# A hybrid attention/SSD block on one core: two gate tiles and two projection tiles computed by halves of 512 tokens, with attention's output loaded a run ahead

## The chip, the cores and the metric

The kernel runs on one core of a Trainium2 chip. The metric is the device time of one execution in microseconds (us). Five engines run in parallel, each through its own list of instructions in order: PE (TensorE, matrix products; PEld is its weight load), ACT (ScalarE), DVE (VectorE), POOL (GpSimd) and SP (SyncE, which here only issues DMA transfers). Engines wait for each other by semaphores.

## The reference

One block over 1024 tokens of width 1024. What matters here is the mixer: a combined input projection feeds an attention branch, an SSD (Mamba-2) branch and two gates; the attention branch's output is projected, gated and merged with the other branch's.

```python
h = rmsnorm(x, pre_norm_mix) * (1.0 + scale_m) + shift_m
proj = h @ w_in
q_lat, kv_lat, k_idx, w_idx, z, xbc, dt_raw, g_a, g_b = jnp.split(proj, IN_SPLITS, axis=-1)
y_a = sparse_mla_attention(q_lat, kv_lat, k_idx, w_idx, positions, ...) @ w_o_attn
y_b = ssd_mixer(z, xbc, dt_raw, ...) @ w_o_ssd
mix = (jax.nn.sigmoid(g_a) * y_a + jax.nn.sigmoid(g_b) * y_b) @ w_out
x = x + gate_m * rmsnorm(mix, post_norm_mix)
```

A feed-forward sub-layer follows.

## The kernel before

Everything is held transposed: 128 features on the partitions, 512 tokens (a half, `b` = 0 or 1) along a row. A product in float32 is made of three products of reduced-precision parts: each operand x is split into hi (ACT rounds it, a copy to float32r) and lo = x - hi (DVE or POOL subtracts). So a tile of 128 outputs by 512 tokens over 1024 inputs is 24 matmuls, called a run here: eight pieces k of the input, three matmuls each. Its weights come in two pieces of four k (`wraw`, loaded by SP; `whi`, ACT; `wlo`, POOL), from a stream W with four buffers of `wraw` and three each of `whi` and `wlo`. A second, single-buffered set `uraw`, `uh`, `ul` (`small_weights`) holds attention's small weights.

The SSD scan goes over 8 groups g and 4 chunks c. Each step (c, g) has four parts of input (`ssd_in`) and, one step later, three of output (`ssd_out`). SP loads `ld` (B, C and x), `al` (the decays) and `zy` (z and d_ea); ACT makes exponentials of `al` and `M`; PE computes `pcb`; DVE masks it (`cbm`) and multiplies `al` and `M` by it; PE transposes x and B (`px`, `pbn`), then does `pyd`, `pst` and `pyo`; DVE and POOL finish `zy`; SP stores it to `d_y`. `ld`, `al` and `zy` share eight buffers (R), so that an `ld` may have to wait until a `d_y` has landed.

Between these parts PE takes steps of six matmuls from a filler, `beside()` (L1124). It first makes eight gate tiles (t = 0 to 7: product `pw`, evicted by ACT to `g`, stored to `d_gb`), from the split input h (`Hs`, in the 32 buffers H), and then attention's projection, eight tiles (product `poa`, evicted by DVE to `ya`, stored to `d_ya`). The projection's input, attention's output `d_att`, is loaded by `at_load` (L1128): SP loads `atl` into one of nine buffers EV, ACT makes `ath`, DVE or POOL the low part, also called `atl`. Four of half 0's eight pieces go to buffers Q; the other four and all of half 1 take over H from h, where they must wait until the gates have read it. PE's order is fixed as the code is written (`in_order`); on the other engines a scheduler sorts by the time at which it expects each instruction's inputs.

Before, the order of runs is gate 6 half 0, gate 6 half 1, gate 7 half 0, gate 7 half 1, then projection tile 0 half 0, tile 0 half 1, and so on. `at_load` stands in the code before gate 7 (four pieces) and after it (twelve).

Of the kernel before, what the change touches and what calls it, by code (L numbers as in the profile page):

```python
# [11 lines left out]
F32R = mybir.dt.float32r  # L12
BF = mybir.dt.bfloat16
AF = mybir.ActivationFunctionType
OP = mybir.AluOpType
# [5 lines left out]
KT = D // P  # L21
# [17 lines left out]
POA_BOTH = 5  # L39
AT_IN_Q = 4  # L40
# [26 lines left out]
def build(tc, a, dbg=None, stop=99, slots=None):  # L67
    nc = tc.nc
    V, S, G, T, SP = nc.vector, nc.scalar, nc.gpsimd, nc.tensor, nc.sync
# [7 lines left out]
    H_ = Arena(ctx, tc, "H", n_slots["H"], 512)  # L77
    Q = Arena(ctx, tc, "Q", n_slots["Q"], 512)
    R = Arena(ctx, tc, "R", n_slots["R"], 1024)
    EV = Arena(ctx, tc, "EV", n_slots["EV"], 512)  # L80
# [4 lines left out]
    def bank_d(name):  # L85
        return pd.tile([P, 512], F32, name=name, tag="d", bufs=3)

    def bank(name):
        return ps.tile([P, 512], F32, name=name, tag="s", bufs=5)

    def f(x):
        return x.bitcast(F32)

    def half(b):
        return slice(512 * b, 512 * b + 512)

    BS = (0, 1)
# [3 lines left out]
    def dump(key, ap, idx=None):  # L101
        if dbg is not None and key in dbg:
            d = dbg[key] if idx is None else dbg[key][idx]
            SP.dma_start(d, ap)
# [19 lines left out]
    def behind(ins):  # L124

        i = ins.ins
        if i.engine in barrier:
            tc.add_manual_dep(i, barrier[i.engine], mybir.DependencyInfo(
                mybir.DependencyClass.NoSync, mybir.DependencyReason.DATA), reason="behind")


    class Stream:
# [21 lines left out]
        def next(self):  # L154
            self.used += 1
            while len(self.tiles) < min(self.used - 1 + self.ahead, len(self.q)):
                self.load()
            return self.tiles[self.used - 1]

    W = Stream("w", 4, n_slots["raw"], n_slots["hi"], n_slots["lo"], n_slots["hi"] - 1)  # L160
    def small_weights(src):

        raw, hi, lo = (wp.tile([P, 4, P], dt, name=tag, tag=tag, bufs=1)
                       for tag, dt in (("uraw", F32), ("uh", F32R), ("ul", F32R)))
        behind(SP.dma_start(raw, src))
        behind(S.activation(hi, raw, AF.Copy))
        behind(G.tensor_tensor(lo, raw, f(hi), op=OP.subtract))
        return hi, lo

    def col_tile(w):  # L170

        kt = w.shape[1]
        return [(w[:, k:k + min(4, kt - k)], min(4, kt - k)) for k in range(0, kt, 4)]
# [27 lines left out]
    d_gb = dr.tile([KT, P, L], F32, name="d_gb")  # L201
    d_att = dr.tile([KT, P, L], F32, name="d_att")
    d_ya = dr.tile([KT, P, L], F32, name="d_ya")
# [25 lines left out]
    def dense_steps(o, b, w, xs, n=6):  # L229

        i = 0
        for (hi, lo), k0, ks in w:
            for j, k in enumerate(ks):
                for wt, xi in ((hi, 0), (hi, 1), (lo, 0)):
                    T.matmul(o, wt[:, k0 + j, :], xs[k][xi][b], start=i == 0, stop=i == 23)  # L235
                    i += 1
                    if i % n == 0 and i < 24:
                        yield

    def wpieces(ks, n=4):  # L240

        return [(W.next(), 0, ks[i:i + n]) for i in range(0, len(ks), n)]

    def split_to(src, hi, lo, lo_eng=None):
        S.activation(hi, src, AF.Copy)  # L245
        (lo_eng or V).tensor_tensor(lo, src, f(hi), op=OP.subtract)  # L246

    def split(alloc, src, name, shape=None, lo_eng=None):
        hi = alloc(name + "h", shape, F32R)
        lo = alloc(name + "l", shape, F32R)  # L250
        split_to(src, hi, lo, lo_eng)
        return hi, lo
# [70 lines left out]
    rx, Hs, first = [None, None], [([None, None], [None, None]) for _ in range(KT)], {}  # L323
# [15 lines left out]
    def k_load(k):  # L339
        raw = EV("p1raw", (P, 3, P))  # L340
        SP.dma_start(raw, a["w_p1"][k])
        ts = [R(f"ada{k}", (P, 4, 256)) for _ in range(2)]
        for i in range(2):
            last = SP.dma_start(ts[i], a["ada_p"][k][i])
        first[k] = ts, raw
        return last
# [9 lines left out]
    def k_h(k, b):  # L356
        x = X0[k][b]
        V.tensor_tensor(x, x, rx[b], op=OP.mult)
        hi, lo = H_(f"h{k}h", dt=F32R), H_(f"h{k}l", dt=F32R)
        i1 = S.activation(hi, x, AF.Identity, bias=mod[:, k:k + 1], scale=amul[:, k:k + 1])  # L360
        V.tensor_scalar(x, x, amul[:, k:k + 1], mod[:, k:k + 1], op0=OP.mult, op1=OP.add)
        i2 = (G if b else V).tensor_tensor(lo, x, f(hi), op=OP.subtract)
        if k == 5:
            barrier.update((i.ins.engine, i.ins.name) for i in (i1, i2))
        Hs[k][0][b], Hs[k][1][b] = hi, lo
        dump("h", x, (k, slice(None), half(b)))

    def k_mm(k, b):
        for i, (wi, xi) in enumerate(((0, 0), (1, 0), (0, 1))):
            for t in range(3):  # L370
                T.matmul(pp1[t][b], first[k][wi][:, t, :], Hs[k][xi][b], start=k == 0 and i == 0, stop=k == KT - 1 and i == 2)
# [14 lines left out]
    with in_order(*ORDERED):  # L386
# [7 lines left out]
        S.activation(rx[0], pr0, AF.Copy)  # L394
        pp1 = [[(bank if t or b else bank_d)(f"pp{t}") for b in BS] for t in range(3)]
        k_h(0, 0)
        k_ada(1)
        x_squares(1, range(4), sums[1])
        k_mm(0, 0)
        k_mod(1)  # L400
        k_h(1, 0)
        x_squares(1, range(4, 8), sums[1])
        k_mm(1, 0)
# [5 lines left out]
        S.activation(rx[1], pr1, AF.Copy)  # L409
        k_mod(2)  # L410
        k_h(0, 1)
        k_h(1, 1)
        k_mm(0, 1)
        k_mm(1, 1)
        for k in range(AHEAD, KT):
            k_h(k, 0)
            k_h(k, 1)
            if k < KT - 1:
                i = k_load(k + 1).ins
# [14 lines left out]
    ks8 = list(range(8))  # L434
# [27 lines left out]
    for b in BS:  # L462
# [5 lines left out]
        hi, lo = Q("ksh", dt=F32R), Q("ksl", dt=F32R)  # L468
# [7 lines left out]
    dt = con.tile([P, NT, 32], F32, name="dt")  # L476
# [77 lines left out]
    for c in range(8):  # L554
# [5 lines left out]
        for hh in range(2):  # L560
            o, oo = 64 * hh, 64 - 64 * hh
            qs = []
            for b in BS:
                t = Q("qs", dt=F32R)
# [35 lines left out]
    for x in range(2):  # L600
# [3 lines left out]
        for j in range(NT):  # L604
# [3 lines left out]
            t = Q("v")  # L608
# [107 lines left out]
    if dbg is not None and "mk" in dbg:  # L716
        for i in MK:
            n = (i + 1) * P
            t = R("t")
# [237 lines left out]
    def gate_steps(c, dst):  # L957

        W.plan(col_tile(a["w_in"][c]))
        w = wpieces(ks8)  # L960
        for b in BS:
            p = bank_d("pw")
            yield from dense_steps(p, b, w, Hs)
            t = EV("g")
            S.activation(t, p, AF.Copy)
            SP.dma_start(dst[:, half(b)], t)
            yield
# [17 lines left out]
    for kind in FILL:  # L985
        if kind == "x":
            conv_group(next(n_x))
        elif kind == "z":
            t = next(n_z)
            gate(1 + t, d_z[t], AF.Silu)  # L990
        else:
            t = next(n_a)
# [121 lines left out]
    def y_load(b, ks, places):  # L1114
        for k in ks:
            t = EV("yl")
            SP.dma_start(t, d_y[k][:, half(b)])
            where = places(k)
            yh, yw = where("yh", dt=F32R), where("yw", dt=F32R)
            S.activation(yh, t, AF.Copy, scale=col("ssd_norm", k))  # L1120
            V.scalar_tensor_tensor(yw, t, col("ssd_norm", k), f(yh), op0=OP.mult, op1=OP.subtract)
            YB[b][k] = ([yh] * 2, [yw] * 2)

    def beside():  # L1124

        AT = [([None, None], [None, None]) for _ in range(KT)]

        def at_load(b, ks, where):  # L1128
            for k in ks:
                t = EV("atl")  # L1130
                SP.dma_start(t, d_att[k][:, half(b)])
                AT[k][0][b], AT[k][1][b] = split(where, t, "at", lo_eng=G if k % 2 else V)

        for t in range(8):
            if t == 7:
                at_load(0, range(AT_IN_Q), Q)
            yield from gate_steps(57 + t, d_gb[t])
        at_load(0, range(AT_IN_Q, KT), H_)
        at_load(1, range(KT), H_)
        for ts, bs in [((t,), BS) for t in range(POA_BOTH)] + [(range(POA_BOTH, 8), (b,)) for b in BS]:  # L1140
            for t in ts:
                W.plan(col_tile(a["w_o_attn"][t]))
                w = wpieces(ks8)
                for b in bs:
                    ya = EV("ya")
                    p = bank_d("poa")
                    yield from dense_steps(p, b, w, AT)
                    V.tensor_copy(ya, p)
                    SP.dma_start(d_ya[t][:, half(b)], ya)
                    yield  # L1150
            if bs == (0,):
                y_load(0, range(12), y_place)

    def y_place(k):
        return Q if k in Y_IN_Q else H_

    filler = beside() if stop != 3 else iter(())
    with in_order(mybir.EngineType.PE):
        prev = None
        for n, s_ in enumerate([(c, g) for g in range(GROUPS) for c in range(NCH)] + [None]):  # L1160
            z = {}
            steps = ([ssd_in(*s_, z)] * 4 if s_ else []) + ([ssd_out(*prev)] * 3 if prev else [])
            k, nf = 0, 4 - n % 2
# [10 lines left out]
    if stop <= 3:  # L1174
        for k in range(16):
            for b in BS:
                t = EV("ydump")
# [333 lines left out]
    with in_order(mybir.EngineType.PE):  # L1511
        AH = a_load(0, [H_] * 16 + [Q] * 6)
        sacc = None
        for t in range(8):
            if t == 4:
                A2 = a_load(1, [Q] * 7 + [R] * 4 + [H_] * 11)
            p = bank("pfo")
# [4 lines left out]
        for t in range(7):  # L1522
            fv[1][t] = H_("fv")
            p = bank("pfo")
# [12 lines left out]
        for c in (slice(0, 256), slice(256, 512)):  # L1537
            p = bank("pfo")[:, 0:256]
# [83 lines left out]
```

## Time and profile before

| | |
|---|---|
| median of three runs | 2433.98 us (2430.88 to 2435.74) |
| profiled execution | 2434.19 us, its span 2432.4 us |
| mean granted PE clock | 0.988 |
| PE busy | 2363.3 us |
| DVE, ACT, POOL busy | 1440.5, 1227.6, 1092.3 us |

A row of a timeline gives the start (us from the span's start), the duration, the engine and the line of the kernel, the operation, output<-inputs with their shapes, and in brackets how long the engine sat idle just before and what ended that (`<-`). In SP's rows (SPq) the duration is that of the issue. A row of the DMA table ends in the median time from issue to landing. Lines in profiles are those of the kernel before.

### The profile page before, as it was taken

To read this page: it belongs to the slowest core of one execution; us is meant where nothing else is said; L and a number is where in the kernel's file an instruction comes from. 1 tells how busy PE (TensorE), PEld (TensorE's weight loads), DVE (VectorE), ACT (ScalarE), POOL (GpSimd) and SP (SyncE) were. 2 spreads that over 40 slices of the span, in tenths; PEclk is the share of its full clock that TensorE was granted. 3 is DMA by queue.
4 is the path that set the end of the run, shared out by engine and by line. 5 is a ranking of instruction groups with operands and counts; after the bars stand their busy time and mean duration, and the time that the engine had idled before them with its cause. 6 is when DMAs were issued, how large, how long until landed. Compare 5 with 4: busy or idle time off the path is not lost.

```text
span 2432.4 us, 34774 instructions
## 1 busy us (share of the span) xinstructions
PE 2363.3 (97%) x11940; PEld 1939.3 (80%) x11940; DVE 1440.5 (59%) x2852; ACT 1227.6 (50%) x2357; POOL 1092.3 (45%) x879
## 2 busy tenths in 40 slices
PE   7999999999999999999998999999999999999998
PEld 5788888888887888788876787888777888888887
DVE  4566776499656666665666774456476666542212
ACT  4346665567445555557666664544454222344432
POOL 2731112222234454552445446557576545444564
PEclk9999999999999999999998999999999999999999
DMA  7224212522213232224778775654465444354642
GB/s 271 87 87 127 70 65 75 165 94 94 98 57 96 94 101 90 92 94 144 227 231 265 232 248 194 220 197 152 158 217 169 160 152 149 119 157 144 205 148 83
DMA packets 219458, 354.37 MB, mean 146 GB/s; under 512 B 21984, under 2 KB 84112, under 8 KB 219280
## 3 DMA queue, kind: packets, MB, share of 16 engines
q1 hardware_dynamic: 218560, 351.56, 44.9%
q8 instruction: 94, 1.54, 0.3%
q14 instruction: 84, 0.69, 0.1%
q10 hardware_dynamic: 720, 0.58, 0.1%
HBM read 267.88 MB, written 87.32 MB: 146 GB/s over the span
## 4 chain that ended last, share of the span: by engine, by line
PE 54%; DVE 5%; DMA 4%; ACT 3%; issue 3%; POOL 2%; SPq 1%; DVEq 0%; POOLq 0%; ACTq 0%
PE p L1346 13%; PE pfo L1478 9%; PE pw L235 7%; PE pos L225 6%; PE plg L777 4%; PE pot L225 3%; PE po L826 2%; PE pt L810 2%; PE poa L235 2%; PE puq L225 2%; DMA d_y<-zy 1%; POOL wr L1340 1%; PE pyd L1074 1%; DMA zy<-d_ea 1%; PE pst L1079 1%
## 5 line engine op out<-in xcount | busy, mean ns | idle before, releaser
L151 POOL TENSOR_TENSOR wlo<-wraw,whi 128x512 fp32r<-128x512 f32 x248 | 341.1, 1377 | 527.3 <-ACT whi L150 455.5
L1346 PE MATMUL p<-xh,wr 128*128 128x512 f32 x880 | 275.0, 391 | 4.3 <-DVE g L1396 4.2
L150 ACT ACTIVATE whi<-wraw 128x512 fp32r<-128x512 f32 x248 | 155.0, 627 | 201.9 <-PE pos L225 43.6
L1478 PE MATMUL pfo<-a,fwh 128*128 128x512 f32 (+1 forms) x684 | 208.6, 386 | 1.0 <-DVE a L246 1.0
L1340 POOL TENSOR_TENSOR wr<-a,wr 128x512 fp32r<-128x512 f32 x110 | 152.6, 1401 | 101.9 <-ACT wr L1339 69.2
L1346 PEld LDWEIGHTS p<-xh,wr 128*128 128x128 f32 x880 | 166.4, 189 | 39.8 <-DVE g L1396 4.6
L1346 PE MATMUL p<-xl,wr 128*128 128x512 f32 x440 | 172.1, 391 | 0.0
L246 POOL TENSOR_TENSOR fwl<-fw,fwh 128x512 fp32r<-128x512 f32 x92 | 114.1, 1244 | 115.9 <-ACT fwh L245 107.3
L1478 PEld LDWEIGHTS pfo<-a,fwh 128*128 128x128 f32 x684 | 127.5, 188 | 27.9 <-DVE a L246 1.9
L789 ACT ACTIVATE lg<-lg,mx 128x256 f32<-128x256 f32 (+7 forms) x128 | 98.9, 773 | 68.0 <-DVE mx L786 67.0
L1478 PE MATMUL pfo<-a,fwl 128*128 128x512 f32 (+1 forms) x342 | 131.9, 386 | 0.0
L1339 ACT ACTIVATE wr<-a 128x512 fp32r<-128x512 f32 x110 | 67.9, 629 | 124.7 <-PE p L1346 97.0
L316 POOL TENSOR_TENSOR adaw<-adaw,cs 128x512 f32<-128x512 f32 x64 | 66.7, 1043 | 132.1 <-DMA adaw<-ada_w 101.6
L245 ACT ACTIVATE fwh<-fw 128x512 fp32r<-128x512 f32 x92 | 54.4, 593 | 124.0 <-PE pfo L1478 102.4
L1346 PE MATMUL p<-h2h,wr 128*128 128x512 f32 x352 | 111.6, 394 | 0.0
L637 ACT ACTIVATE junk<-acc,cand__2203 128x1024 bf16<-128x1024 f32 (+2 forms) x96 | 86.2, 898 | 45.8 <-DVE cand__2203 L680 29.9
L225 PE MATMUL pos<-yh,wlo 128*128 128x512 f32 x256 | 100.9, 394 | 1.4 <-POOL wlo L151 1.3
L588 DVE SCALAR_TENSOR_TENSOR acc<-rel,widx,acc 128x384 f32<-128x384 f32 (+2 forms) x90 | 87.1, 988 | 24.8 <-ACT rel L583 24.7
L583 ACT ACTIVATE rel<-prel 128x512 f32<-128x512 f32 (+3 forms) x160 | 77.1, 523 | 48.4 <-PE prel L582 44.9
L225 PE MATMUL pos<-yh,whi 128*128 128x512 f32 x256 | 100.6, 393 | 0.4 <-ACT whi L150 0.4
L225 PE MATMUL pos<-yw,whi 128*128 128x512 f32 x256 | 100.6, 393 | 0.0
L1346 PEld LDWEIGHTS p<-xl,wr 128*128 128x128 f32 x440 | 83.2, 189 | 17.3
(572 smaller groups left out, 6886.4 us busy)
## 6 DMA issues: line engine op xcount, KB each, us to landing
wraw<-w_in SPq DMA_DIRECT2D x130, 256.0 KB, 2.9
a<-w_ffn_in SPq DMA_DIRECT2D x124, 256.0 KB, 3.4
fw<-w_ffn_out SPq DMA_DIRECT2D x80, 256.0 KB, 2.7
adaw<-ada_w SPq DMA_DIRECT2D x64, 256.0 KB, 3.0
al<-d_ac SPq DMA_DIRECT2D x32, 512.0 KB, 5.9
wraw<-w_o_ssd SPq DMA_DIRECT2D x64, 256.0 KB, 3.2
al<-d_a SPq DMA_DIRECT2D x44, 256.0 KB, 5.4
d_a<-g SPq DMA_DIRECT2D x40, 256.0 KB, 2.3
```

The source lines that it names most:

```text
L150: behind(S.activation(hi[:, :kt], raw[:, :kt], AF.Copy))
L151: behind(G.tensor_tensor(lo[:, :kt], raw[:, :kt], f(hi[:, :kt]), op=OP.subtract))
L225: T.matmul(o, wt[:, k0 + i, :], xs[k][xi][b][:, sl], start=pi == 0 and i == 0 and wt is hi and xi == 0, stop=pi == len(pcs) - 1 and i == l ...
L235: T.matmul(o, wt[:, k0 + j, :], xs[k][xi][b], start=i == 0, stop=i == 23)
L246: (lo_eng or V).tensor_tensor(lo, src, f(hi), op=OP.subtract)
L588: V.scalar_tensor_tensor(acc[i][:, 0:n], rel[:, 0:n], ws, acc[i][:, 0:n], op0=OP.mult, op1=OP.add)
L637: S.activation(jk, y, AF.Sign, scale=-1.0, bias=a_, accum_out=o)
L777: T.matmul(p[:, 0:w2], st[qi], KVT[ki][:, o_:o_ + w2], start=x == 0, stop=x == 2)
L789: S.activation(lg[:, 0:n], lg[:, 0:n], AF.Exp, scale=-1.0, bias=m, accum_out=rr[:, 2 * t + hh:2 * t + hh + 1])
L1340: G.tensor_tensor(w[:, 1], src, f(w[:, 0]), op=OP.subtract)
L1346: T.matmul(p, w[:, wi, i], X[x][i][xi], start=start and i == 0 and k == 0, stop=i == 3 and k == 2, skip_group_check=True)
L1478: T.matmul(p, w[wi][:, k - k0], xs[k][xi][:, sl], start=k == 0 and i == 0, stop=k == FT - 1 and i == 2)
```

## The change

It makes the last two gate tiles as a pair, by halves: gate 6 half 0, gate 7 half 0, gate 6 half 1, gate 7 half 1; likewise the first two tiles of the projection. A pair needs four weight pieces at once; three come from W, the fourth from the small set (`two_tiles`). Loads of attention's output are split from their conversion: `at_load` issues four loads, and `at_split`, one run later, converts them, with ACT's conversions bound to stand after the last eviction (`anchor`, an order on ACT without a semaphore). There are four such batches of four. The projection's tile 0 is evicted by ACT instead of DVE. The buffers of h are taken half by half, so that those of half 0 come free together.

```diff
-        hi, lo = H_(f"h{k}h", dt=F32R), H_(f"h{k}l", dt=F32R)
+        hi, lo = HB[b][k]
...
+    HB = [[(H_(f"h{k}h", dt=F32R), H_(f"h{k}l", dt=F32R)) for k in range(KT)] for b in BS]
...
         def at_load(b, ks, where):
-            for k in ks:
-                t = EV("atl")
+            raws = [EV("atl") for k in ks]
+            for t, k in zip(raws, ks):
                 SP.dma_start(t, d_att[k][:, half(b)])
-                AT[k][0][b], AT[k][1][b] = split(where, t, "at", lo_eng=G if k % 2 else V)
+            return b, ks, where, raws
+
+        def at_split(b, ks, where, raws):
+            for t, k in zip(raws, ks):
+                hi, lo = where("ath", dt=F32R), where("atl", dt=F32R)
+                i = S.activation(hi, t, AF.Copy).ins
+                tc.add_manual_dep(i, ahead[0], ...)
+                (G if k % 2 else V).tensor_tensor(lo, t, f(hi), op=OP.subtract)
+                AT[k][0][b], AT[k][1][b] = hi, lo
...
+        def anchor(ins):
+            ahead[0] = ins.ins.name
...
+        def gate_run(t, b, w):
+            p = bank_d("pw")
+            yield from dense_steps(p, b, w, Hs)
+            g = EV("g")
+            anchor(S.activation(g, p, AF.Copy))
+            SP.dma_start(d_gb[t][:, half(b)], g)
+            yield
+
+        def poa_run(t, b, w):
...
+            if t:
+                V.tensor_copy(ya, p)
+            else:
+                anchor(S.activation(ya, p, AF.Copy))
...
+        def two_tiles(src, ts):
+            W.plan(col_tile(src[ts[0]]) + col_tile(src[ts[1]])[:1])
+            return [wpieces(ks8), [(W.next(), 0, ks8[:4]), (small_weights(src[ts[1]][:, 4:8]), 0, ks8[4:])]]
...
-        for t in range(8):
-            if t == 7:
-                at_load(0, range(AT_IN_Q), Q)
+        for t in range(6):
             yield from gate_steps(57 + t, d_gb[t])
-        at_load(0, range(AT_IN_Q, KT), H_)
-        at_load(1, range(KT), H_)
...
+        ld = at_load(0, range(AT_IN_Q), Q)
+        w = two_tiles([a["w_in"][57 + t] for t in range(8)], (6, 7))
+        yield from gate_run(6, 0, w[0])
+        at_split(*ld)
+        yield from gate_run(7, 0, w[1])
+        ld = at_load(0, range(AT_IN_Q, KT), H_)
+        yield from gate_run(6, 1, w[0])
+        at_split(*ld)
+        ld = at_load(1, range(4), H_)
+        yield from gate_run(7, 1, w[1])
+        at_split(*ld)
+        ld = at_load(1, range(4, KT), H_)
+        w = two_tiles(a["w_o_attn"], (0, 1))
+        yield from poa_run(0, 0, w[0])
+        at_split(*ld)
+        yield from poa_run(1, 0, w[1])
+        for i in range(2):
+            yield from poa_run(i, 1, w[i])
```

In the changed file the SSD's lines stand two further down, the splits are L1139 (ACT) and L1142 (DVE, POOL), the evictions `g` L1154.

On ACT, from the SSD step around the first split on, before:

```order
L1097 ACTIVATE ysqt<-zy 128x512
L1024 ACTIVATE M<-al,acum 128x128 x4
L245 ACTIVATE ath<-atl 128x512
L1025 ACTIVATE al<-al,acum 128x256 x4
L1027 ACTIVATE M<-M 128x512
L245 ACTIVATE ath<-atl 128x512
L965 ACTIVATE g<-pw 128x512
L1027 ACTIVATE al<-al 128x1024
L245 ACTIVATE ath<-atl 128x512
L150 ACTIVATE whi<-wraw 128x512
L245 ACTIVATE ath<-atl 128x512
```

The same engine two steps earlier in the program, now:

```order
L1154 ACTIVATE g<-pw 128x512
L1139 ACTIVATE ath<-atl 128x512
L1029 ACTIVATE al<-al 128x1024
L1139 ACTIVATE ath<-atl 128x512 x3
L1099 ACTIVATE ysqt<-zy 128x512
L1026 ACTIVATE M<-al,acum 128x128 x4
L1027 ACTIVATE al<-al,acum 128x256 x4
L1029 ACTIVATE M<-M 128x512
```

The first four splits moved from amid a step's exponentials to behind an eviction, two steps before.

On SP, where the last twelve loads are issued, before:

```order
L1019 DMA al<-d_ac 128x1024
L1131 DMA atl<-d_att 128x512
L1094 DMA d_y<-zy 128x2x256
L1131 DMA atl<-d_att 128x512
L966 DMA d_gb<-g 128x512
L1131 DMA atl<-d_att 128x512 x8
L1065 DMA zy<-d_z 128x2x256
L1068 DMA zy<-d_ea 64x2x256 x2
L1131 DMA atl<-d_att 128x512
L1013 DMA ld<-d_bc 128x2x256
```

On SP, the second and third batch of four, now:

```order
L1016 DMA ld<-d_xs 128x2x256
L1133 DMA atl<-d_att 128x512 x2
L1155 DMA d_gb<-g 128x512
L1133 DMA atl<-d_att 128x512 x2
L1021 DMA al<-d_ac 128x1024
L149 DMA wraw<-w_o_attn 128x512
L1096 DMA d_y<-zy 128x2x256
L1067 DMA zy<-d_z 128x2x256
L1015 DMA ld<-d_bc 128x2x256
L1016 DMA ld<-d_xs 128x2x256
L1133 DMA atl<-d_att 128x512 x4
L1021 DMA al<-d_ac 128x1024
```

Twelve loads that stood within two steps are now spread over three, four ahead of an `al` each time.

On ACT, at the end of attention (`rb` scales an output of attention, `qh` is the last query tile's hi part), now:

```order
L791 ACTIVATE lg,rr<-lg,mx 128x384
L817 ACTIVATE pc<-pt 128x2x128
L791 ACTIVATE lg,rr<-lg,mx 128x512 x2
L831 ACTIVATE rb<-po 128x256
L166 ACTIVATE uh<-uraw 128x512
L752 ACTIVATE qh<-puq 128x512
```

The `uh` there is new: the fourth piece of the gates' pair is converted some 150 us before its use, ahead of `qh`.

More of the change, by code (lines that the diff above doesn't have):

```diff
@@ L1139, in beside @@
-        at_load(1, range(KT), H_)
-        for ts, bs in [((t,), BS) for t in range(POA_BOTH)] + [(range(POA_BOTH, 8), (b,)) for b in BS]:
+            return b, ks, where, raws
[3 more added lines that the diff above has]
+                i = S.activation(hi, t, AF.Copy).ins
+                tc.add_manual_dep(i, ahead[0], mybir.DependencyInfo(
+                    mybir.DependencyClass.NoSync, mybir.DependencyReason.DATA), reason="behind")
+                (G if k % 2 else V).tensor_tensor(lo, t, f(hi), op=OP.subtract)
+                AT[k][0][b], AT[k][1][b] = hi, lo
@@ new lines, in beside @@
+        ahead = [None]
+        def anchor(ins):
[8 more added lines that the diff above has]
+        def poa_run(t, b, w):
+            ya = EV("ya")
+            p = bank_d("poa")
+            yield from dense_steps(p, b, w, AT)
+            if t:
+                V.tensor_copy(ya, p)
+            else:
+                anchor(S.activation(ya, p, AF.Copy))
+            SP.dma_start(d_ya[t][:, half(b)], ya)
+            yield
@@ new lines, in beside @@
+        ld = at_load(0, range(AT_IN_Q, KT), H_)
[11 more added lines that the diff above has]
+            yield from poa_run(i, 1, w[i])
+        for ts, bs in [((t,), BS) for t in range(2, POA_BOTH)] + [(range(POA_BOTH, 8), (b,)) for b in BS]:
@@ L1144, in beside @@
                 for b in bs:
[L1145 to L1150, printed above, removed]
+                    yield from poa_run(t, b, w)
             if bs == (0,):
```

## The prediction

> **What bounds the kernel now.** I read the page's busy shares first, then the windows table around the lines that change, then the instructions in order of time on PE, ACT, DVE and SP in the two bad windows, and last the DMA table.
>
> ```profile
> PE 2363.3 (97%) x11940; PEld 1939.3 (80%) x11940; DVE 1440.5 (59%) x2852; ACT 1227.6 (50%) x2357; POOL 1092.3 (45%) x879
> ```
>
> PE is busy 97% of the span, so a change elsewhere pays only where PE waits or is slowed after a wait. The changed lines stand between 1255 and 1354 us. In the windows table the first numbers are the width and PE's busy time, the last three PE's granted clock, the DMA share and GB/s.
>
> ```profile
> core 0: us, PE busy (x) PEld busy (x) DVE busy (x) ACT busy (x) POOL busy (x), PEclk, DMA share, GB/s
> 1210.00:1225.00 15.00, 13.58 (x75) 11.19 (x74) 12.57 (x19) 13.13 (x33) 7.40 (x5) 1.00 0.70 211
> ...
> 1255.00:1287.90 32.90, 32.90 (x188) 26.60 (x185) 20.21 (x32) 20.64 (x48) 11.15 (x10) 1.00 0.78 243
> 1287.90:1300.60 12.70, 7.94 (x37) 4.92 (x35) 10.25 (x15) 11.22 (x25) 8.65 (x6) 0.73 0.85 259
> 1300.60:1310.10 9.50, 9.50 (x56) 7.67 (x55) 3.65 (x7) 3.98 (x10) 3.62 (x3) 1.00 0.74 209
> 1310.10:1323.90 13.80, 9.37 (x24) 5.87 (x24) 9.27 (x11) 8.76 (x16) 8.79 (x6) 0.63 1.04 367
> 1323.90:1354.00 30.10, 30.10 (x179) 24.16 (x179) 25.22 (x37) 20.33 (x48) 16.47 (x12) 1.00 0.67 215
> ```
>
> Two windows stand out: PE idles 12.70 - 7.94 = 4.76 us in the first and 13.80 - 9.37 = 4.43 us in the second, and in both its clock drops, to 0.73 and 0.63. Everywhere else here PE is full at clock 1.00. What the windows cost in all is read from PE's rows, against the same work a step earlier.
>
> ```profile
> 1265.84 1.03 PE L1084 MATMUL pyo<-ld,state 128*128 128x256 f32 x4
> 1270.48 0.47 PE L235 MATMUL pw<-h4h,whi 128*128 128x512 f32 x1
> 1280.20 0.60 PE L1041 MATMUL px<-ident,ld 128*128 128x128 f32 x4
> 1284.60 0.58 PE L235 MATMUL pw<-h6h,whi 128*128 128x512 f32 x1
> 1288.99 0.66 PE L1041 MATMUL px<-ident,ld 128*128 128x128 f32 x4 [0.65 <-DVE zy L1087]
> 1293.56 0.69 PE L1050 MATMUL pbn<-ident,ld 128*128 128x128 f32 x2 [2.53 <-ACT bn L1052]
> 1295.27 1.11 PE L1074 MATMUL pyd<-al,X 128*64 128x256 f32 x2 [1.02 <-DVE al L1035]
> 1300.58 0.58 PE L235 MATMUL pw<-h4h,whi 128*128 128x512 f32 x1
> 1310.15 1.03 PE L1084 MATMUL pyo<-ld,state 128*128 128x256 f32 x4
> 1312.98 0.50 PE L235 MATMUL poa<-ath,whi 128*128 128x512 f32 x1 [1.80 <-ACT ath L245]
> 1319.78 0.80 PE L235 MATMUL poa<-atl,whi 128*128 128x512 f32 x1 [1.69 <-DVE atl L246]
> 1323.94 0.48 PE L235 MATMUL poa<-ath,whi 128*128 128x512 f32 x1
> ```
>
> First stall: from px (due at 1288.99 - 0.65 = 1288.34) to the projection at 1300.58 is 12.24 us; the step before did the same (px, pbn, six projections, pyd, one block of four) from 1280.20 to 1284.60 in 4.40. It costs 7.84 us. Second: pyo, twelve projections, pcb and px take 1310.15 to 1323.94, 13.79 us, against 1265.84 to 1270.48, 4.64, for the same work. It costs 9.15 us. Together 16.99, of which 9.19 is idle and 7.8 the slow clock.
>
> The cause is on ACT and DVE, which take instructions in order.
>
> ```profile
> 1283.42 1.26 ACT L1024 ACTIVATE M<-al,acum 128x128 f32<-128x128 f32 x4
> 1286.98 0.63 ACT L245 ACTIVATE ath<-atl 128x512 fp32r<-128x512 f32 x1 [2.30 <-DMA atl<-d_att]
> ...
> 1312.30 0.63 ACT L245 ACTIVATE ath<-atl 128x512 fp32r<-128x512 f32 x1 [5.21 <-DMA atl<-d_att]
> ```
>
> ```profile
> 1292.23 0.77 DVE L246 TENSOR_TENSOR atl<-atl,ath 128x512 fp32r<-128x512 f32 x1 [2.38 <-ACT ath L245]
> 1292.92 0.55 DVE L1033 TENSOR_TENSOR cbm<-pcb,mask 128x384 f32<-128x384 f32 x1
> 1312.96 0.69 DVE L246 TENSOR_TENSOR atl<-atl,ath 128x512 fp32r<-128x512 f32 x1 [6.07 <-ACT ath L245]
> ```
>
> A split of attention's output stands on ACT ahead of the SSD's exponentials and waits 2.30 us for its load; the DVE half waits 2.38 us behind it, and cbm, al and M, which pyd needs, come after that. The second time the waits are 5.21 and 6.07 us, and there poa needs the split tiles themselves. The loads were issued too late:
>
> ```profile
> 1255.73 0.34 SPq L149 DMA_DIRECT2D wraw<-w_o_attn  x1
> 1263.27 0.38 SPq L1013 DMA_DIRECT2D ld<-d_bc  x1
> 1282.65 2.69 SPq L1131 DMA_DIRECT2D atl<-d_att  x4
> 1308.40 7.24 SPq L1131 DMA_DIRECT2D atl<-d_att  x8
> ```
>
> ```profile
> atl<-d_att SPq DMA_DIRECT2D x16, 256.0 KB, 5.6
> d_y<-zy SPq DMA_DIRECT2D x10, 256.0 KB, 6.1
> ```
>
> **The change part by part.** PE's work is the same in kind, number and order; only names differ (uh for whi in eight pieces of six projections, and tile 7 before tile 6's second half). Any gain is waits and clock.
>
> (1) First four loads. They move on SP from behind the ld at 1282 to behind the wraw at 1255.73, their splits on ACT to behind the eviction that now runs here:
>
> ```profile
> 1265.47 0.58 ACT L965 ACTIVATE g<-pw 128x512 f32<-128x512 f32 x1
> 1269.47 0.59 PE L1030 MATMUL pcb<-ld 128*128 128x256 f32 x2
> ```
>
> First load: issued by about 1256.1 + 0.7, landed 5.6 later at 1262.4. Last: d_y, d_gb and four issues of 2.69 / 4 = 0.67 us later, at 1259.5, landed at 1265.1. The first split comes at 1265.47 + 0.58 = 1266.05. Slack 0.9 to 3.7 us: the stall at 1284 to 1287 on ACT goes. Credit 7.84.
>
> (2) The other twelve. Before they went out in one run, eight of them taking 7.24 us of SP. Now they go four at a time, at the places of 1282, 1294 and 1305, one run before use, and the first twelve splits stand ahead of poa's first half. Half 0 of h is released two runs earlier (tile 7's first half runs second), so the H buffers are free. Credit 9.15.
>
> (3) What SP now has in front of the SSD's loads. Twelve loads (batches one, three and four) stand ahead of zy, al or d_y where none stood. Price: from 0.67 us each (the row of x4) to 7.24 / 8 = 0.91 under load; per batch 2.7 to 3.6 us. What covers it: for batch one the next ld waits anyway for d_y to land (issued at 1256.2, ld at 1263.27), and pcb uses ld 6.2 us after that issue, little more than a landing takes. For al, behind batch three, there is about none, since its user moves 7.84 us earlier. So 0 to 3.6 us a batch comes out on PE, 0 to 10.9 in all. I take 1 us a batch, 3 in all, nearer the low end because the waits that SP causes without such a batch show as 1.42 us (15.00 - 13.58 above) and as the 1.14 below.
>
> (4) DVE's order in the place of the first stall: the split now stands between X and al, so al comes about 1 us after pyd could start. Nearest row:
>
> ```profile
> 1381.34 0.66 PE L1074 MATMUL pyd<-al,X 128*64 128x256 f32 x4 [1.14 <-DVE al L1035]
> ```
>
> I take 1, bounds 0 and 1.7 (the longest DVE wait above). Another 1 for the SSD's own loop, which had 17 us more to recover in; bounds 0 and 1.42 + 1.14 = 2.6.
>
> (5) The small weights. One load goes out near 1056 and one near 1113, and uh, 0.63 us like ath, is put on ACT ahead of qh:
>
> ```profile
> 1111.19 0.60 ACT L750 ACTIVATE qh<-puq 128x512 fp32r<-128x512 f32 x1 [1.51 <-PE puq L225]
> 1112.68 0.48 PE L777 MATMUL plg<-kvth,qh 128*128 128x512 f32 x1
> ```
>
> qh ends at 1111.79 and plg starts 0.89 later, so 0.63 is hidden: 0, at most 0.63. Two evictions of poa move from DVE to ACT, which is half idle: 0. Weights of poa's tile 2 wait for tile 0's second half to end, one run before use. From 1270.48 to 1284.60 (rows above) lie one and a quarter runs, so a run lasts 11 us; two whi like ath take 1.3 us and two wlo 2.8:
>
> ```profile
> L151 POOL TENSOR_TENSOR wlo<-wraw,whi 128x512 fp32r<-128x512 f32 x248 | 341.1, 1377 | 527.3 <-ACT whi L150 455.5
> ```
>
> They fit: 0.
>
> Sum: -7.84 - 9.15 + 3 + 1 + 1 = -11.99. The profiled execution takes 2434.19 (2432.4 span, 1.8 around it), against a median of 2433.98, 0.2 apart. 2434.2 - 12.0 = 2422.2, so **2422 us**. With every price at zero it is 2417.2; with all at their ends, 10.9 + 1.7 + 2.6 + 0.6 = 15.8, it is 2433.0.
>
> [...] The rows: no PE wait exceeds 2.53 us, and yet the clock is 0.73 and 0.63; the 1.42 us idle in the window from 1210 leave it at 1.00. So several short waits close together slow it, single ones of 1 us do not, and what I leave in (3) and (4) is priced without it. [...]
>
> **The rivals.** (A) The DMA side becomes the bound. From the windows, width by share from 1255 to 1354 adds to 32.90 x 0.78 + 12.70 x 0.85 + 9.50 x 0.74 + 13.80 x 1.04 + 30.10 x 0.67 = 78.0 us of DMA time in 99.0. Take 17 out of the span and it is 78.0 in 82.0, 95%. For it: at 1.04 the loads crawled. Against: 13.80 us at 1.04 carried the run of loads that is now spread, and two weight loads have left the stretch. Then (3) goes to its end: -16.99 + 10.9 + 2 = -4, 2430.
>
> (B) Slower: head-of-line blocking comes back in more places. Four batches are now anchored behind evictions; if each lands after its eviction ACT stands still four times, not twice. 2.30 us of ACT wait cost 7.84, so four cost 31.4, less the 17.0 removed: +14.4, 2449. It decides at three batches late (23.5 - 17.0 = +6.5, 2441), and a batch is late if its landing takes 0.9 to 3.7 us longer than 5.6. For it: 95% DMA share. Against: SP issues them a run early.
>
> (C) It does not do what it says: PE's stalls belong to the loop from d_y to ld (the ld at 1263.27 waited for d_y) and the splits merely stood in the gap. Against: that loop ran through 1255 to 1287.9 with PE at 32.90 of 32.90. Then 2434.
>
> **How the numbers follow.** Forecast 0.66, own range 2417 to 2427; A 0.18, 2427 to 2433; B 0.08; C 0.08. The range 2415 to 2433 takes in the forecast (its low end with the 1.14 at 1381 gone too and 1 for noise) and A, and leaves out B, C and a few hundredths. 0.2% is 4.9 us, about what a measurement here can tell (the three runs spread over 4.86): faster is below 2429.1, all of the forecast and 0.11 of A, 0.77; same is the rest of A and C, 0.15; slower is B, 0.08.
>
> **What would show it.** Right: in the changed trace ACT's waits for atl vanish or fall under 1 us, PE runs at clock 1.00 through the gates' last runs and poa's first, px to the next projections takes about 4.4 us, and poa's rows name neither ath nor atl as releaser. (3) shows as SP waiting for landings around the four batches, with PE waits of about 1 us at pcb or pyd. A shows as a DMA share near 1 for 60 us and landings above 6 us; B as ACT waits for atl at g or ya; C as the same idle with DVE or ACT waiting for ld. Wrong would make it above all a landing late by more than 3.7 us at the first batch, or clusters of short waits that pull the clock down again.

## The result and the profile after

The changed kernel took 2420.59 us (median of five, 2416.99 to 2425.55), the kernel before 2432.34 in the runs beside it (2430.88 to 2435.74). The ratio is 0.9949, 95% interval 0.9933 to 0.9964: 11.8 us faster. A second measurement of the same kernel (below) gave 2422.68 and 0.9957, 0.9940 to 0.9974. The sum of the forecast was 11.99. Three runs far above all others, one of e12 (2926.06 us) and two of the kernel before beside later experiments (8909.27 and 12718.71 us), are in no median or ratio here.

The profiled execution is the slowest of its five, 2425.55 us, with a span of 2423.8 and a mean PE clock of 0.990. PE's share is still 97%:

```profile
PE 2361.5 (97%) x11940; PEld 1940.9 (80%) x11940; DVE 1437.8 (59%) x2850; ACT 1227.9 (51%) x2359; POOL 1092.2 (45%) x879
```

The windows around the change, after (columns as in the prediction):

```profile
1240.00:1287.00 47.00, 47.00 (x271) 37.98 (x271) 35.24 (x56) 30.28 (x70) 21.34 (x17) 1.00 0.90 278
1287.00:1298.00 11.00, 7.60 (x41) 5.99 (x40) 10.09 (x12) 10.63 (x24) 7.53 (x6) 0.84 0.81 248
1298.00:1313.00 15.00, 15.00 (x85) 12.07 (x85) 12.85 (x16) 10.90 (x24) 10.59 (x8) 1.00 0.97 319
```

The second bad window is gone: from 1298 to 1328 PE is full at clock 1.00. The first is not: 3.40 us idle and a clock of 0.84 remain, in one wait. PE's waits over 0.6 us, in this stretch and in the 100 us behind it:

```profile
1292.96 0.66 PE L1076 MATMUL pyd<-al,X 128*64 128x256 f32 x4 [3.40 <-DVE al L1037]
1356.76 0.67 PE L1032 MATMUL pcb<-ld 128*128 128x256 f32 x2 [1.55 <-DMA ld<-d_bc]
1423.85 1.09 PE L1032 MATMUL pcb<-ld 128*128 128x256 f32 x2 [2.06 <-DMA ld<-d_bc]
```

ACT now finds its inputs there: of the waits of 2.30 and 5.21 us for `atl` one of 1.14 is left.

```profile
1264.27 0.63 ACT L1139 ACTIVATE ath<-atl 128x512 fp32r<-128x512 f32 x1
...
1313.51 0.63 ACT L1139 ACTIVATE ath<-atl 128x512 fp32r<-128x512 f32 x1 [1.14 <-DMA atl<-d_att]
```

The loads land no sooner (5.7 us after their issue, 5.6 before). They are issued sooner: the last of the first batch at about 1256.5 (1255.75 and half of 1.43), 7.8 us ahead of ACT's first split, where before the batch went out from 1282.65 and ACT wanted it from 1284.7 on.

```profile
1255.75 1.43 SPq L1133 DMA_DIRECT2D atl<-d_att  x2
```

To weigh each stall apart I use three `pcb` matmuls as marks: the one ahead of both stalls, the one between them, and the one behind. Their rows before, and after:

```profile
1241.79 0.60 PE L1030 MATMUL pcb<-ld 128*128 128x256 f32 x2
...
1303.52 0.59 PE L1030 MATMUL pcb<-ld 128*128 128x256 f32 x2
...
1340.99 0.59 PE L1030 MATMUL pcb<-ld 128*128 128x256 f32 x2
```

```profile
1240.97 0.60 PE L1032 MATMUL pcb<-ld 128*128 128x256 f32 x2
...
1299.77 0.59 PE L1032 MATMUL pcb<-ld 128*128 128x256 f32 x2
...
1328.07 0.59 PE L1032 MATMUL pcb<-ld 128*128 128x256 f32 x2
```

From the first to the second mark it was 61.73 us and is 58.80: the first stall gave back 2.93 of its 7.84. From the second to the third it was 37.47 and is 28.30: 9.17, all of the second stall's 9.15. Together 12.1. The first mark itself came between 1233.96 and 1244.22 in the fourteen traces of this study, in code that the kernels share almost to the line. The two profiles of one and the same kernel differ there by 1.0 us (before) and 2.1 us (changed); how the rest divides between kernels and chance was not measured. So a whole run carries up to 10 us from ahead of the place of the change, and the marks tell more than the medians.

### The profile page after: what moved, and what is told of

Read it like the earlier page. It is cut to its first block, busy times and chain, and to the rows that moved or that the text cites. A ratio compares the mean times of both kernels' runs of the same rounds, so it can differ in the third digit from the quotient of the medians.

```text
span 2423.8 us, 34772 instructions
## 1 busy us (share of the span) xinstructions
PE 2361.5 (97%) x11940; PEld 1940.9 (80%) x11940; DVE 1437.8 (59%) x2850; ACT 1227.9 (51%) x2359; POOL 1092.2 (45%) x879
## 4 chain that ended last, share of the span: by engine, by line
PE 60%; DVE 4%; DMA 2%; ACT 2%; issue 2%; POOL 1%; SPq 0%; DVEq 0%; POOLq 0%; ACTq 0%
PE p L1394 16%; PE pfo L1526 9%; PE pw L235 8%; PE pos L225 6%; PE plg L779 4%; PE pot L225 3%; PE po L828 2%; PE pt L812 2%; PE poa L235 2%; PE puq L225 2%; PE pyd L1076 1%; PE pst L1081 1%; PE pyo L1086 1%; DMA zy<-d_ea 0%; PE pyd L1077 0%
```

## The experiments

The table gives the gain on the first profile of before between the marks (first stall, second stall), the further gain from the third mark to the `pcb` at 1433.13 in before, and the whole time. Each whole time stands beside its own runs of before (medians of 2431.9 to 2433.7).

| kernel | first (of 7.84) | second (of 9.15) | to 1433 | median, us | ratio to before, 95% |
|---|---|---|---|---|---|
| before, second profile | 1.79 | -0.05 | 0.55 | 2431.90 | 0.9994 (0.9977 to 1.0011) |
| changed, first profile | 2.93 | 9.17 | -3.63 | 2420.59 | 0.9949 (0.9933 to 0.9964) |
| e1 changed again | 3.12 | 9.17 | 0.51 | 2422.68 | 0.9957 (0.9940 to 0.9974) |
| e2 pairs, no early loads | -0.94 | 2.64 | 0.31 | 2431.30 | 0.9986 (0.9969 to 1.0003) |
| e3 early loads, no pairs | 3.83 | 8.97 | -2.95 | 2421.25 | 0.9960 (0.9943 to 0.9977) |
| e4 no anchor | -5.29 | 9.17 | -1.40 | 2429.74 | 0.9983 (0.9971 to 0.9995) |
| e5 no loads | 3.05 | 9.15 | 0.03 | 2421.16 | 0.9948 (0.9934 to 0.9962) |
| e6 one split | 6.51 | 7.74 | -1.78 | 2420.91 | 0.9950 (0.9931 to 0.9968) |
| e7 before, first batch early | 1.99 | 0.82 | 0.55 | 2426.59 | 0.9977 (0.9965 to 0.9989) |
| e9 ysqt behind | 0.78 | 2.74 | -3.07 | 2431.22 | 0.9994 (0.9980 to 1.0007) |
| e12 batch two behind this al | 3.22 | 9.11 | -2.39 | 2422.89 | 0.9966 (0.9954 to 0.9978) |
| e11 batch two a step later | 5.97 | 6.89 | -3.38 | 2425.60 | 0.9974 (0.9961 to 0.9986) |
| e13 = e3, batch two later | 7.52 | 1.81 | -0.05 | 2424.91 | 0.9977 (0.9964 to 0.9990) |

**e1, the changed kernel again.** No edit.

> The changed kernel once more, unaltered. Theory F (the forecast's: ScalarE's splits stood waiting for loads in front of the SSD's exponentials, loads a run ahead end that): 2418 to 2424 us, 0.9930 to 0.9965 of before, ACT's waits for atl together under 2 us. What was left in the first profile should come again if it belongs to the kernel and not to the one execution: a wait of about 3.4 us at pyd near 1293 (behind al on DVE), and pcb's waits for ld of about 1.5 and 2 us near 1357 and 1424. If those at 1357 and 1424 do not come again, they are chance, and the profiled execution of 2425.6 us was that much above the median for them.

PE's only wait over 0.6 us between 1240 and 1438 in its timeline:

```profile
1290.72 1.12 PE L1076 MATMUL pyd<-al,X 128*64 128x256 f32 x4 [3.27 <-DVE al L1037]
```

The wait at `pyd` came again, 3.27 us; so it belongs to the kernel. `pcb`'s two waits for `ld` did not: from the third mark on this execution ran 0.51 us better than before, the first 3.63 worse. Those 4.1 us are most of what set the first profile's 2425.55 above this one's 2418.99.

**e2, pairs without early loads.**

```diff
-        ld = at_load(0, range(AT_IN_Q), Q)
...
         yield from gate_run(6, 0, w[0])
-        at_split(*ld)
+        at_split(*at_load(0, range(AT_IN_Q), Q))
```
(and likewise at the other three places)

> The pairs, the small weights, the order of h's buffers, the evictions and the anchor stay; each batch of four is loaded at the place of its splits in place of a run ahead. Theory F: each batch waits on ACT for an issue and a landing (5.7 us and 0.7 an issue), less the 3 to 5 us that ACT has to spare; ACT's waits for atl of 2 to 8 us come back at two to four places, the time is 2432 to 2450, no better than before. Theory P (the order of the tiles by halves, which frees h's buffers two runs earlier, is what pays): 2419 to 2425, as the changed kernel.

ACT's longest waits in its timeline, one at each of three batches:

```profile
1273.46 0.63 ACT L1139 ACTIVATE ath<-atl 128x512 fp32r<-128x512 f32 x1 [6.82 <-DMA atl<-d_att]
...
1302.48 0.63 ACT L1139 ACTIVATE ath<-atl 128x512 fp32r<-128x512 f32 x1 [4.57 <-DMA atl<-d_att]
...
1324.86 1.35 ACT L1139 ACTIVATE ath<-atl 128x512 fp32r<-128x512 f32 x2 [3.73 <-DMA atl<-d_att]
```

ACT stands for its loads again and 10.4 of the 12.1 us are lost. 2431.30 is just under the 2432 to 2450 that F gave; P is out.

**e3, early loads without pairs.**

```diff
-        w = two_tiles([a["w_in"][57 + t] for t in range(8)], (6, 7))
-        yield from gate_run(6, 0, w[0])
+        w = one_tile(a["w_in"][57 + 6])
+        yield from gate_run(6, 0, w)
         at_split(*ld)
-        yield from gate_run(7, 0, w[1])
+        yield from gate_run(6, 1, w)
...
```

> Loads four at a time a run ahead, splits behind the anchored evictions, the new order of h's buffers and tile 0 evicted by ACT all stay; the gate tiles 6 and 7 and the projection's tiles 0 and 1 go back to the order of before (tile by tile, both halves, all weights from W). Theory F: 2418 to 2425, within 0.15% of the changed kernel, since every split is still ready before its use. Theory P: the splits of the second half come a run late for the projection, poa waits for ath and atl as before (1.8 and 1.7 us and a slow clock, 9.15 us in all): 2428 to 2432.

The gain is there in full, 12.8 us between the marks. So the tiles by halves, which give the change its name, are not needed for it; four loads at a time, a run ahead, are (e2).

**e4, without the anchor.** The line with `tc.add_manual_dep` is left out of `at_split`.

> The changed kernel without the order on ACT that puts the splits behind the last eviction; the scheduler then puts the second batch's splits one SSD step earlier, behind the eviction of gate 7's first half, and the third and fourth batch one step earlier too. Theory F: those loads have one run less, so ACT waits 2 to 6 us for atl at one to three places, ahead of exponentials: 2424 to 2436. Rival O (the loads ahead are enough, the order on ACT is idle ornament): 2418 to 2424.

ACT at the second batch, and PE behind it:

```profile
1283.66 1.25 ACT L1139 ACTIVATE ath<-atl 128x512 fp32r<-128x512 f32 x2 [5.96 <-DMA atl<-d_att]
```

```profile
1299.05 1.13 PE L1076 MATMUL pyd<-al,X 128*64 128x256 f32 x4 [8.68 <-DVE al L1037]
```

As F had it: the scheduler moves the second batch's splits a step up, ACT meets loads issued only at 1278 to 1282, and everything that it should have done for the SSD stands behind them. One wait of 5.96 us on ACT became one of 8.68 on PE. The order on ACT is worth 8 us: without it the early loads keep 3.88 of the 12.1 us between the marks.

**e5, no loads.** All sixteen loads are left out, the splits read a constant.

```diff
-            raws = [EV("atl") for k in ks]
-            for t, k in zip(raws, ks):
-                SP.dma_start(t, d_att[k][:, half(b)])
-            return b, ks, where, raws
+            return b, ks, where, [ones[:, None, :].to_broadcast([P, 4, P]) for k in ks]
...
```

> The changed kernel with all sixteen loads of attention's output left out; ACT's, DVE's and POOL's splits stay where they are and read a constant tile instead (so the projection's input is left out). It prices term (3) of the forecast, what the loads cost the SSD's own loads on SP and the DMA engines. Forecast's term: 3 us faster than the changed kernel (2420.6 and 2422.7 in two measurements), 2417 to 2420. Theory L (pcb's waits for ld after 1350 come from the SSD's own loop and by chance): within 1 us of it, 2420 to 2424. Rival A (the DMA side is the bound): 7 to 11 us faster, 2411 to 2415. In each case the 3.3 us wait at pyd near 1291 should stay if its chain has no load in it (zy on POOL, ysqt, M and al on ACT), and go if it has.

The third of the windows shown above, and PE's wait:

```profile
1298.00:1313.00 15.00, 15.00 (x92) 12.11 (x91) 12.87 (x15) 10.89 (x23) 9.44 (x8) 1.00 0.69 211
```

```profile
1292.11 0.66 PE L1076 MATMUL pyd<-al,X 128*64 128x256 f32 x4 [3.27 <-DVE al L1037]
```

The DMA share falls from 0.97 to 0.69 in that window, and no time goes with it: 12.20 us between the marks, against 12.10 and 12.29 with the loads. The wait at `pyd` is 3.27 us, as in e1. So the loads cost the stretch nothing, and theory L has it.

**e6, one split.** One load and one split in place of sixteen; the projection reads that one tile throughout.

> The changed kernel with one load and one split in place of sixteen (the projection multiplies the same split tile sixteen times; fifteen loads and splits are left out): the ceiling of what handling this input can cost. Stall 1 cost 7.84 us before, of which the change got 3.0 to 3.1. Theory S (what is left of it is the splits' own time: ath between g and al on ACT, atl between X and al on DVE): pyd's wait of 3.3 us near 1291 falls to 0 to 1, the time to 2415 to 2418. Rival Z (what is left is ACT waiting for ysqt's input, zy from POOL, ahead of the next exponentials): the wait falls only by the 1.1 us of those two instructions, to about 2.2, the time to 2418 to 2422.

The `pyd` that waited 3.3 to 3.4 us, here:

```profile
1283.98 0.66 PE L1076 MATMUL pyd<-al,X 128*64 128x256 f32 x4 [1.42 <-DVE al L1037]
```

The same wait is 1.42 us, between S (0 to 1) and Z (2.2), with the clock at 1.00, and the first stall gives back 6.51. The second gives back 7.74, with a wait of 1.19 us at `pcb` for `zy`. In the whole time none of it shows.

**e7, before with the first batch early.**

```diff
...
+            if t == 6:
+                ld = at_load(0, range(AT_IN_Q), Q)
             if t == 7:
-                at_load(0, range(AT_IN_Q), Q)
+                at_split(*ld)
...
```

> The kernel before with one part of the change: the first four loads are issued two runs earlier (ahead of gate 6), their splits stay ahead of gate 7; no pairs, no anchor, the other twelve as before. Theory F: stall 1 loses what it lost in the changed kernel, 3 us, as ACT finds its inputs there; stall 2 (9.15 us) stays with its waits of 5.2 us on ACT for atl and of 1.7 to 1.8 us at poa: 2430 to 2432, 0.9975 to 0.9995 of before. Rival (stall 1 is only pushed on by the splits' position amid the exponentials): no gain, 2433 to 2435.

1.99 us of the first stall, not 3. ACT no longer waits for these loads, yet PE's waits behind the splits are there (1.28 at `pbn`, 1.33 and 1.03 at `pyd`). The second stall stays but for 0.82. The whole time, 2426.59, lies under both forecasts: 5.8 us below before, interval 2.7 to 8.5. The marks account for 3.36 of it, up to 1433; this profile is also 5.77 us ahead at the first mark (1236.02 against 1241.79), where nothing was changed.

**Before once more.** No edit.

> The kernel before once more, unaltered, for a second profile of it. Theory F: the two stalls belong to the program and not to one execution: px to the next projection near 1289 takes 11 to 13 us, pyo to px near 1310 takes 13 to 14.5, with ACT's waits for atl of about 2 and 5 us, 16 to 18 us together; and the time up to 1240 differs by up to 8 us from the first profile, as it did between the kernels that are the same up to there. Rival E (the stalls of the first profile were a bad execution): under 12 us together.

PE's waits in the first stall:

```profile
1292.48 0.44 PE L1050 MATMUL pbn<-ident,ld 128*128 128x128 f32 x2 [1.28 <-ACT bn L1052]
1294.25 0.65 PE L1074 MATMUL pyd<-al,X 128*64 128x256 f32 x2 [1.33 <-DVE al L1035]
1295.93 0.32 PE L1075 MATMUL pyd<-M,X 128*64 128x128 f32 x1 [1.03 <-DVE M L1035]
```

The second stall is the same (0.05 apart). The first is 1.79 us shorter, because here ACT's splits found their loads landed; what is left of it, 6.05, shows the same three waits as e7. So the two come to 15.25 us in this execution, under the 16 to 18 expected, and of the first stall's 7.84 only about 1.8 was waiting for loads. Most of the rest goes with the work of four splits in that step, ready or not: without a split there, 1.33 us (e6), 1.87 (e11, below) or 0.32 (e13, below) are lost.

**e9, ysqt moved.** From gate 6 to projection tile 1, `ysqt` is bound behind the next step's `al` exponential.

```diff
...
+            i = S.activation(sq, yt, AF.Square).ins
+            if behind_:
+                tc.add_manual_dep(i, behind_, ...)
...
```

> The changed kernel; from gate 6 to the projection's tile 1, ysqt (the square of a step's zy) is bound on ACT to stand behind the next step's exponentials of al in place of ahead of M's. Rival Z (ACT's wait of 3.4 to 5.6 us for POOL's zy at ysqt delays the exponentials and so pyd): the 3.3 us wait at pyd near 1291 falls under 1 us, PE's clock stays 1.00 there, 4 to 5 us faster than the changed kernel: 2416 to 2419. Theory S (the splits' own time): the wait stays over 2.3 us, 2420 to 2423.

ACT, and PE behind it, right after the binding begins:

```profile
1254.14 0.99 ACT L1043 ACTIVATE M<-al,acum 128x128 f32<-128x128 f32 x3 [3.83 <-DMA al<-d_ac]
```

```profile
1262.76 1.13 PE L1095 MATMUL pyd<-al,X 128*64 128x256 f32 x4 [5.83 <-DVE al L1056]
```

As a way to gain time it fails. With `ysqt` out of the way ACT came to the next exponentials too early and stood 3.83 us for their `al`, with `zy`'s eviction behind them; PE then waited 5.83. It is the mistake of the kernel before in another place.

For the `pyd` that Z spoke of the run does not decide. There, PE has no wait, as Z said, and no slow matmul (`pst` right behind takes 1.13 us, as it does in windows at clock 1.00):

```profile
1290.98 0.66 PE L1095 MATMUL pyd<-al,X 128*64 128x256 f32 x4
```

From the `pcb` ahead of it to the next (1288.20 to 1296.22) it is 8.02 us, against 13.06 in the first profile of the changed kernel and 15.98 before. But the second batch's splits had left that step's exponentials too: ACT stood 6.39 us for an `al` and came to them only at 1294.18. The table's 0.78 is this step's gain of 7.96 less 7.18 lost around the wait at 1262.

**e12, e11, e13: the second batch's splits later.**

```diff
+                exps.append(i.ins.name)
...
         yield from gate_run(6, 1, w[0])
+        ahead[0] = exps[-2]
         at_split(*ld)
```
(e12; in e11 the last exponential of `al`, a step later, in e13 the same in e3's order of tiles)

> The changed kernel with the second batch's splits bound on ACT behind the al exponential that follows the eviction: one ath (0.52 us from start to start) leaves the place between g and that exponential, one atl on DVE (0.6 us) the place between X and al; nothing else moves. Theory S (what is left of stall 1 is the splits' own time): the 3.3 us wait at pyd near 1291 falls by 1.1 to about 2.2 us, and with the slow clock behind it 1 to 2.5 us are gained: stretch 1240 to 1345 gains 13.3 to 15 us on before in place of 12.1 to 12.3. Rival D (DVE works slowly beside POOL there: al 2.06 us where 1.22 is usual, zy's last step 1.99 where 0.88 is): the wait stays at 2.7 to 3.3.

> As the run before, but behind the al exponential of the step after (three of four splits leave the stretch of stall 1, and all stand 8 us later, one half run ahead of their use). Theory S: as the run before or up to 1 us better at pyd near 1291, if the splits still come in time for the projection's first half (k = 4 to 7, near 1303): 2417 to 2420. Rival B' (a split too late costs more than one too early): poa waits for ath or atl 1 to 2 us near 1303 and the time is 2421 to 2427.

> The kernel with loads a run ahead but the order of tiles of before (2421.3 in its first run), with the second batch's splits bound behind the al exponential of the step after: no pairs, no small weights. Theory S and F together (loads ahead and splits clear of the exponentials are all that matters): 2417 to 2420, no slower than any kernel so far. If the pairs matter after all, once the second batch is later: poa waits for ath or atl near 1303, 2422 to 2428.

e12's `pyd` in PE's timeline and the window around it, then e11's:

```profile
1290.65 0.66 PE L1079 MATMUL pyd<-al,X 128*64 128x256 f32 x4 [2.01 <-DVE al L1040]
```

```profile
1286.00:1297.00 11.00, 8.99 (x46) 7.11 (x45) 10.44 (x13) 11.00 (x24) 8.55 (x6) 0.84 0.78 261
```

```profile
1294.78 0.66 PE L1079 MATMUL pyd<-al,X 128*64 128x256 f32 x4 [1.96 <-DVE al L1040]
```

```profile
1290.00:1300.00 10.00, 8.04 (x50) 6.58 (x49) 9.11 (x12) 10.00 (x23) 7.19 (x5) 1.00 0.81 255
```

In e12 the wait fell by 1.3 us to 2.01, as S said and D did not, but the stretch gained only 12.33, not the 13.3 to 15 that S gave: another wait of 0.92 came at 1280.54, and the clock stayed low (0.84). In e11 the wait is the same, the clock is 1.00, and the first stall gives back 5.97. In e13 `pyd` does not wait at all there and 7.52 of 7.84 come back. But both pay later, in e11 at `pyd`, where ACT stands 2.62 us for the last of the sixteen loads (issued at 1313.89) ahead of the exponentials, in e13 at `poa`:

```profile
1325.33 0.66 PE L1079 MATMUL pyd<-al,X 128*64 128x256 f32 x4 [1.63 <-DVE al L1040]
```

```profile
1308.49 0.50 PE L235 MATMUL poa<-ath,whi 128*128 128x512 f32 x1 [1.44 <-ACT ath L1142]
```

In whole time none of the three beats the changed kernel. Up to the third mark e11 is 0.6 to 0.8 us ahead of it, with 12.86.

## Why the prediction was right, and where it was right by luck

The time is right, and the sum too: 11.99 forecast, 12.1 and 12.3 between the marks. The terms are not.

- **(2), credit 9.15: right.** 9.17 in both profiles, and lost again when the loads were late (e2: 2.64) or the splits (e13: 1.81). The order of the tiles, which the prediction names for h's buffers, was not needed: 8.97 without it (e3).
- **(1), credit 7.84, with (4), 1 us of DVE order: mis-sized.** Net 6.84 was expected, 2.93 to 3.12 came. The step that failed is the cause given for the first stall, ACT's wait for loads. Before's second profile and e7 bound that wait at about 2 us (1.79 and 1.99); e11, e6 and e13 show that without any split in that step 6.0 to 7.5 come back. The change took the first batch's splits out of the step and put the second batch's in. The prediction priced that at 1, "bounds 0 and 1.7", without the clock; what stayed lost is 4.7 to 4.9 (7.84 less what came back): a wait of 3.3 to 3.4 us and about 1.5 of slow clock (0.84 in the window of either profile). Where the wait arises is seen in the rows of PE, ACT, DVE and POOL in the first profile of the changed kernel, and beside them in e6, without splits:

```profile
1287.36 0.60 PE L1043 MATMUL px<-ident,ld 128*128 128x128 f32 x4
```

```profile
1283.54 0.63 ACT L1099 ACTIVATE ysqt<-zy 128x512 f32<-128x512 f32 x1 [3.57 <-POOL zy L1095]
...
1288.63 0.63 ACT L1139 ACTIVATE ath<-atl 128x512 fp32r<-128x512 f32 x1
1289.15 1.05 ACT L1029 ACTIVATE al<-al 128x1024 f32<-128x1024 f32 x1
```

```profile
1287.76 1.39 DVE L1037 TENSOR_TENSOR M<-M,cbm 128x512 f32<-128x512 f32 x1 [0.52 <-ACT M L1029]
1289.07 0.55 DVE L1035 TENSOR_TENSOR cbm<-pcb,mask 128x384 f32<-128x384 f32 x1
1289.54 0.67 DVE L1045 TENSOR_TENSOR X<-px,dt 128x512 f32<-128x512 f32 x1
1290.14 0.70 DVE L1142 TENSOR_TENSOR atl<-atl,ath 128x512 fp32r<-128x512 f32 x1
1290.76 2.06 DVE L1037 TENSOR_TENSOR al<-al,cbm 128x1024 f32<-128x1024 f32 x1
```

```profile
1290.29 1.45 POOL L1056 TENSOR_TENSOR Xd<-X,decay 128x512 f32<-128x512 f32 x1
```

  The same in e6, PE and then DVE:

```profile
1280.35 0.60 PE L1043 MATMUL px<-ident,ld 128*128 128x128 f32 x4
```

```profile
1281.99 0.67 DVE L1045 TENSOR_TENSOR X<-px,dt 128x512 f32<-128x512 f32 x1
1282.59 1.24 DVE L1037 TENSOR_TENSOR al<-al,cbm 128x1024 f32<-128x1024 f32 x1
```

  PE was ready at 1289.56. Counted from `px`, `X` starts 2.18 us later, in e6 1.64: 0.54 more. Then `atl` holds the multiplication by 0.62, and that takes 2.06 us where e6's takes 1.24, 0.82 more. With the 1.42 us that e6 waits without a split this gives 3.40, the whole wait. The same sum gives 3.26 for e1 (3.27 measured), and for e11 and e12, where no `atl` stands there and `al` takes 1.23, 1.97 and 2.02 (1.96 and 2.01).

  So the split's own part of the wait is 1.44. The exponential, held up 0.52 us by `ath`, ends at 1290.20, while DVE is still at `atl`: on ACT the split costs next to nothing. The 0.54 is Z's part (of e6 and e9), by the rows and not by a run of its own: DVE waits there for ACT's `M`, and ACT had waited 3.57 us at `ysqt` for POOL's `zy` (2.63 in e6). The 1.42 is DVE's order: `cbm` and `X`, both for the next step, stand ahead of `al`. In e13 DVE takes `al` first, at 1290.29 with `cbm` behind it at 1291.43, and `pyd` does not wait. Whether that order could be had in the changed kernel was not tried.
- **(3), 3 us for SP and the DMA side: not seen.** e5 prices the loads at 0.1 us or less. `pcb`'s waits for `ld` behind 1350 come with the loads and without (e6: 1.86 us at 1347.90), and stay away with them (e1). What makes them come was not found.
- **The 1 us for the SSD's own loop** is the same waits: 0 in e1, 3.6 and a slow clock (0.83 from 1421 to 1431) in the first profile, over its bound of 2.6.
- **(5), 0:** nothing in the traces speaks against it; e3, without the small weights, is as fast. It was not measured by itself.

So a credit too large by 3.8 met charges too large by 4 (3 and 1): that the sum came out is luck. Rival A is out (0.97 in a window where PE is full at clock 1.00, and e5). So is C: the stalls come and go with loads and splits (e2, e6). B did not come in this kernel but is real: e2 and e4 are that mechanism, and 5.96 us of it on ACT cost 8.68 on PE.

Of the signs to look for, `poa` names neither `ath` nor `atl`, and ACT's waits are nearly gone (1.14, a little over the 1 us set). The clock is not 1.00 through, and from `px` to the next projections it takes 8.72 us (1287.36 to 1296.08), not 4.4: that is the sign that (1) was too large. The sign set for (3), a wait at `pcb`, came 50 us behind the batches, and in e6 without them.

## What to carry to other kernels

A wait that ends on a load need not cost what the window around it costs: read the same window in an execution where the load was in time, or leave the work out and see what stays. On an engine that works in order, take both steps together: issue a load a whole unit of work ahead, and fix the place of the instruction that uses it behind something that is certain to come later. Work moved out of a bad step goes somewhere; count it against the step it lands in, with what it does to its neighbours there (0.62 us of `atl` on DVE cost 1.44).

## What the runs showed of the hardware

**The clock.** Single waits of PE of 1.42 (e6), 1.63 and 1.96 us (both e11) left windows of 10 to 19 us at 1.00. One of 2.01 us, 8 us after one of 0.92, came with a clock of 0.84 in an 11 us window (e12), one of 2.06 at `pcb` with 0.83 in a 10 us window (1421 to 1431 in the first profile of the changed kernel); waits of 3.27 to 3.40 came with 0.84 too, one of 5.83 with 0.90 over 15 us (e9), one of 8.68 with 0.67 over 9 us (e4). Before's second profile has no wait above 1.33 us in its first stall, but three within 4 us (1.28, 1.33, 1.03), and `pst` right behind them takes 1.80 us, against 1.13 in the steps around it (1274.57 and 1308.42). So the length of one wait does not decide alone: a single one of 1.96 us left the clock at 1.00, and three of at most 1.33 went with slow matmuls. What else decides was not found.

**DVE beside POOL.** In the rows above `al` starts on DVE 0.47 us after `Xd` on POOL and takes 2.06 us, `Xd` 1.45. In e6 `al` starts first, in 1.24 us, and `Xd` pays:

```profile
1282.74 1.99 POOL L1056 TENSOR_TENSOR Xd<-X,decay 128x512 f32<-128x512 f32 x1
```

`Xd` takes 1.99, against 1.04 a few steps on in the same trace. So in these two steps the one that started second took 0.82 (`al`) or 0.95 us (`Xd`) longer. It is `atl` that makes `al` second: in e12, where `atl` stands behind `al`, `al` takes 1.23. Why the one that starts second takes longer no run shows.
